# Splitting w_o in the queue of the other late weights, beside the w_in products, instead of in the chunk stage

## The chip, the cores and the metric

The kernel runs on one core of a Trainium2 chip. A core has a matrix engine (TensorE, PE in the profile), a vector engine (VectorE, DVE), a scalar engine (ScalarE, ACT), GpSimd (POOL) and SyncE (SP), which here only issues transfers. Each engine works through its own list of instructions in order. Transfers are issued from the lists of SP and ACT (SPq and ACTq in the profile) and run on 16 shared DMA engines. The metric is the device time of one execution in microseconds, the median of several runs.

## The reference, cut to what matters

One layer of a decoder is computed for a prompt of 1024 rows and for 64 sample rows (8 sequences of 8):

```
h = rmsnorm(x) * (1 + scale) + shift
[u_pool | z_pool | z_ssm | xBC | dt | g] = h @ w_in
P = (pool_mix(u_pool) * silu(z_pool)) @ w_pool_out        # 512 -> 1024
S = gated_rmsnorm(SSD(conv(xBC)) + D*x, z_ssm) @ w_ssm_out # 2048 -> 1024
x = x + gate * ((sigmoid(g_pool) * P + sigmoid(g_ssm) * S) @ w_o)   # w_o: 1024 x 1024
y = rmsnorm(x)
```

All data are float32. SSD is a state recurrence that runs over chunks of 128 rows, for four groups of heads.

## The kernel before, in words

**Halves.** A product of full accuracy is made of three products of rounded numbers: each weight tile is split into a high half (the rounded tile) and a low half (the tile less its rounded self), and each activation likewise; then high x high, high x low and low x high are accumulated. ACT makes the high half by a copy, and GpSimd makes the low half by a subtraction.

**Stages.** In the profile's time the stages follow one another like this.
- Up to about 95 us: the norm, the modulation, the first products (`first`).
- 95 to about 535 us: 20 pairs of column blocks of w_in (`pair`, `strassen`): each pair is seven products on PE, and after each product `run_units` calls `beside` once; that is one step. In this stage the pairs belong to the convolution and the pooling (DVE does their element work), with some plain gates between them. For each pair ACT and GpSimd also split seven w_in tiles (`split`, lines 155 to 163; tiles `whi` and `wlo`, four buffers each); their raw data arrive in `rawA` by SP's queue.
- 535 to about 800 us: ten more pairs of w_in, with the sample rows' recurrence beside them.
- About 830 to 1110 us: the chunk stage. 32 chunks (4 groups x 8) are woven with 32 product units (`pieces`) that multiply by w_pool_out and by three quarters of w_ssm_out; PE's list is written out in order there.
- From 1110 us: the last quarter of w_ssm_out, the gates, and the product with w_o.

**The queue of late weights.** `splits` (lines 408 to 447) splits the weights that are needed only in the chunk stage or after it and puts both halves into DRAM: 8 tiles of w_pool_out and 32 of w_ssm_out, each 128 x 512. A job has three parts. `begin` takes a buffer `pw` (two exist) and loads the raw tile by ACT's queue. `halve` makes the high half on ACT into the buffer `ph` (one exists) and stores it by ACT's queue, then the low half on GpSimd in place in `pw`; a tile of w_ssm_out is scaled by four ACT instructions first. `end` stores the low half by SP's queue. Job n begins at step 17n/5, is halved three steps and ended five steps after that. The steps are those of the 20 pairs between 95 and 535 us. A transfer that waits for a buffer or for data holds everything behind it in the list of its engine.

**w_o.** `wo_splits` (lines 1663 to 1677) does the same for w_o in the chunk stage: 16 tiles of 128 x 512, the raw tile loaded by SP's queue, the high half made on ACT and stored by ACT's queue, the low half made on GpSimd and stored by SP's queue. Two raw buffers and one `ph` exist here as well. It is called twice for each chunk from chunk 13 on, and what the lists' planner makes of that lies between 840 and 992 us. `wo_prep` loads the halves back from DRAM after 1130 us.

**Order.** A planner orders the instructions of each engine from the order of the program, priorities and estimated times; `behind` and `paced` tie some transfers and copies to earlier instructions.

Of the kernel before, what the change touches and what calls it, by code (L numbers as in the profile page):

```python
# [8 lines left out]
F32 = mybir.dt.float32  # L9
F32R = mybir.dt.float32r  # L10
AF = mybir.ActivationFunctionType
ALU = mybir.AluOpType
# [8 lines left out]
P = 128  # L21
D = 1024
# [7 lines left out]
NG = 4  # L30
# [16 lines left out]
def tile_pool_ssd_step(  # L47
# [6 lines left out]
    nc = tc.nc  # L54
    uid = [0]

    def nm(s):
        uid[0] += 1
        return f"{s}_{uid[0]}"
# [45 lines left out]
    load = nc.sync.dma_start  # L105
    store_ = nc.scalar.dma_start
    mm = nc.tensor.matmul
    act = nc.scalar.activation
# [225 lines left out]
    def in_line(engines, begin=False):  # L334
        traced = nc.cur_bb.bb.instructions
        for i in traced[len(traced) if begin else line[0]:]:
            if i.engine in engines:
                if i.engine in line[1]:
                    tc.add_manual_dep(i, line[1][i.engine], mybir.DependencyInfo(
                        mybir.DependencyClass.NoSync, mybir.DependencyReason.DATA), reason="in_line")  # L340
                line[1][i.engine] = i.name
        line[0] = len(traced)
# [42 lines left out]
    def dram(name, shape, dt=F32):  # L385
        return dr.tile(list(shape), dt, tag=name, name=name)
# [10 lines left out]
    wp_d = [dram(f"wp{m}", [P, 2, 4, P]) for m in range(8)]  # L397
    ws_d = [[dram(f"ws{g}{m}", [P, 2, 4, P]) for m in range(8)] for g in range(NG)]

    def behind(engine, n=0):  # L400

        of = (i for i in reversed(nc.cur_bb.bb.instructions) if i.engine == engine)
        for _ in range(n):
            next(of)
        return tc.issue_after(next(of))


    def splits():
        jobs = [(w_pool_out[0, :, m * P:(m + 1) * P], None, wp_d[m]) for m in range(8)]
        jobs += [(w_ssm_out[0, g * 512:(g + 1) * 512, m * P:(m + 1) * P], 24 + 4 * g, ws_d[g][m])  # L410
                 for g in range(NG) for m in range(8)]
        raws, made = {}, [0]

        def paced():

            return highs[min(made[0] + 3, len(highs) - 1)]

        def begin(n):
            raws[n] = gas[0].tile([P, 4, P], F32, tag="pw", name=nm("pw"), bufs=2)
            with tc.issue_after(paced()):  # L420
                store_(raws[n], jobs[n][0].rearrange("(k p) c -> p k c", p=P))

        def halve(n):
            raw, gain = raws[n], jobs[n][1]
            hi = gas[0].tile([P, 4, P], F32R, tag="ph", name=nm("ph"), bufs=1)
            with tc.issue_after(paced()):
                if gain is not None:
                    for k in range(4):
                        act(raw[:, k], raw[:, k], AF.Copy, scale=vT[:, gain + k:gain + k + 1])
                act(hi, raw, AF.Copy)  # L430
                store_(jobs[n][2][:, 0], hi.bitcast(F32))
            nc.gpsimd.tensor_tensor(raw.bitcast(F32R), raw, hi.bitcast(F32), ALU.subtract)

        def end(n):
            with behind(mybir.EngineType.SP):
                load(jobs[n][2][:, 1], raws.pop(n))
        at = {}
        for n in range(len(jobs)):
            for f, step in ((end, 5), (begin, 0), (halve, 3)):
                at.setdefault(n * 17 // 5 + step, []).append((f, n))  # L440
        for t in range(max(at) + 1):
            made[0] += 1
            for f, n in sorted(at.get(t, ()), key=lambda x: x[1]):
                f(n)
            yield
# [254 lines left out]
    def between(n):  # L700
        with behind(mybir.EngineType.DVE):
            if n != 3:
                step()
            if n in (3, 4, 5) and prep_q:
                next(prep_q[0], None)
            while n == 6 and later:
                step()
# [32 lines left out]
    gas = []  # L740
# [634 lines left out]
    def sample_end(g):  # L1375
        sz = ckt([P, 4, P], "sz", 3)[:, :, :NS]
        load(sz, z_d[g][:, :, SEQ:])
        v = ckt([P, 4, P], "v")[:, :, :NS]
        load(v, ys_d[g])
        finish(g, SEQ, NS, v, sz)  # L1380
# [148 lines left out]
    def pool_rows():  # L1529
        with behind(mybir.EngineType.SP):  # L1530
            load(new_pool_s[0, :, 0:7, :], state_pool[0, :, 8:15, :])

    first()
    units = [plain(to_conv), light[1], plain(pool_rows)]
    units += weave(heavy, light[2:-LAST])
    pre = splits()
    units.append(plain(lambda: [None for _ in pre]))
    units.append(plain(to_ssd))
# [64 lines left out]
    ck = right.__enter__()  # L1603
# [48 lines left out]
    def pieces():  # L1652
        ws = first_ws
        nxt = len(ws)
        for i, (pf, run) in enumerate(prods):
            while nxt < len(prods) and nxt <= i + 1:
                ws[nxt] = prods[nxt][0]()
                nxt += 1
            yield from run(ws.pop(i))
    pc_ = pieces()  # L1660
    wo_d = [dram(f"wo{k}", [P, 2, D]) for k in range(8)]

    def wo_splits():
        raws = {}
        for n in range(18):
            if n < 16:
                raws[n] = ck.tile([P, 512], F32, tag="pw", name=nm("pw"), bufs=2)
                load(raws[n], w_o[0, n // 2 * P:n // 2 * P + P, n % 2 * 512:n % 2 * 512 + 512])
            if n > 1:
                load(wo_d[(n - 2) // 2][:, 1, n % 2 * 512:n % 2 * 512 + 512], raws.pop(n - 2))  # L1670
            yield
            if n < 16:
                hi = ck.tile([P, 512], F32R, tag="ph", name=nm("ph"), bufs=1)
                act(hi, raws[n], AF.Copy)
                store_(wo_d[n // 2][:, 0, n % 2 * 512:n % 2 * 512 + 512], hi.bitcast(F32))
                nc.gpsimd.tensor_tensor(raws[n].bitcast(F32R), raws[n], hi.bitcast(F32), ALU.subtract)
            yield
    wos = wo_splits()
    RATE = 2.56
    FRONT = 4  # L1680

    def products(t):

        nonlocal made
        while made < RATE * t:
            next(pc_, None)
            made += 1
# [5 lines left out]
        next(pc_)  # L1693
    next(seq[0])
    for i in range(len(seq)):
        if i > 12:
            next(wos, None)
        if i + 1 < len(seq):
            with behind(mybir.EngineType.DVE, 1 - i) if i < 2 else ExitStack():
                next(seq[i + 1])  # L1700
        products(i + 0.4)
        if i > 0:
            next(seq[i - 1], None)
        if i > 12:
            next(wos, None)
        next(seq[i], None)
        if i % NC == 3:
            sample_end(i // NC)
        if i + 3 < len(seq):
            next(seq[i + 3])  # L1710
        if i + 2 < len(seq):
            with behind(mybir.EngineType.Activation) if i == 0 else ExitStack():
                next(seq[i + 2])
        products(i + 1.0)
    next(seq[-1], None)
    for it in (pc_, wos):
        for _ in it:
            pass
    in_line((mybir.EngineType.PE,))
    right.__exit__(None, None, None)  # L1720
    while right_all:
# [16 lines left out]
    for c in range(9):  # L1738
        n = min(P, T - c * P)
# [5 lines left out]
    for c in range(9):  # L1745
        n = min(P, T - c * P)
# [4 lines left out]
    wo, mh, ml = [None] * 8, [None] * 8, [None] * 8  # L1751
# [90 lines left out]
    for half in range(2):  # L1842
        c = slice(half * 512, half * 512 + 512)
# [102 lines left out]
```

## Time and profile before

| | |
|---|---|
| median of 3 runs | 1297.37 us (1296.57 to 1301.63) |
| span of the profiled execution, first to last instruction | 1297.1 us |
| granted clock of PE, mean over the span | 0.999 |
| busy PE / DVE / ACT / POOL | 1255.9 / 910.5 / 708.8 / 677.4 us |
| moved by DMA | 251.70 MB, mean 194 GB/s |

The profile is that of one execution. Its span is the time that it gives for that execution. The page lists busy time by engine, the span in slices, the DMA queues, the chain of work that ended last, and groups of instructions by source line. Views of the same trace give busy time in chosen stretches, what each engine waited for, single instructions in order of time, and all instructions that touch a tile. In a row of single instructions the numbers are start, duration, engine, line, operation and shape; what stands in brackets is the idle time of the engine before it and what ended it. In a row of a tile the numbers are the count, then shortest, median and longest duration in ns, then first and last start.

### The profile page before, as it was taken

The numbers are of one execution on the slowest core, as the hardware profiler recorded it, in microseconds if no ns is written. First come the engines' busy times: TensorE is split into PE (matmuls) and PEld (weight loads), VectorE is DVE, ScalarE is ACT, GpSimd is POOL, SyncE is SP. The second block draws the span as 40 slices with busy tenths as digits, with TensorE's granted clock in tenths as the row PEclk, the third lists the DMA queues.
The fourth block names the chain that finished last, engine by engine and source line by source line (L and its number), as shares of the span: only waits on it lengthen the run. The fifth ranks groups of instructions, "written<-read, shape, count | busy, mean of one in ns | idle before, by whom it ended". The sixth has DMA issues, their size and how long they took to land.

```text
span 1297.1 us, 26554 instructions
## 1 busy us (share of the span) xinstructions
PE 1255.9 (97%) x9771; PEld 1173.9 (90%) x9771; DVE 910.5 (70%) x1580; ACT 708.8 (55%) x1684; POOL 677.4 (52%) x563
## 2 busy tenths in 40 slices
PE   7999999999999999999999999999998999999998
PEld 6779999989999999999889999889998999999786
DVE  4685778866979578775777665488676888576433
ACT  4665356375656564545455453687987868201111
POOL 1007668677869776664344444276776747314000
PEclk9999999999999999999999999999999999999999
DMA  9837345465455544444656555999988656575631
GB/s 326 259 107 224 119 150 173 142 202 170 146 180 197 165 155 133 161 135 129 181 158 173 152 178 164 356 355 354 338 270 262 202 168 199 172 266 159 226 106 52
DMA packets 233795, 251.70 MB, mean 194 GB/s; under 512 B 31265, under 2 KB 177905, under 8 KB 233658
## 3 DMA queue, kind: packets, MB, share of 16 engines
q1 hardware_dynamic: 161568, 171.60, 42.1%
q10 hardware_dynamic: 72098, 78.41, 17.5%
q8 instruction: 77, 1.26, 0.4%
q14 instruction: 52, 0.43, 0.1%
HBM read 167.06 MB, written 83.01 MB: 193 GB/s over the span
## 4 chain that ended last, share of the span: by engine, by line
PE 67%; issue 8%; DMA 8%; DVE 6%; POOL 5%; ACT 4%; SPq 0%; ACTq 0%; POOLq 0%; DVEq 0%
PE ps L603 6%; PE ps L604 6%; PE ps L605 6%; PE mm L603 6%; PE mm L605 6%; PE mm L604 6%; PE mm L355 3%; PE mm L356 3%; PE mm L354 3%; PE ps L1208 2%; PE ps L1892 2%; PE ps L1894 2%; PE ps L1893 2%; POOL wlo L163 2%; PE ps L1211 2%
## 5 line engine op out<-in xcount | busy, mean ns | idle before, releaser
L163 POOL TENSOR_TENSOR wlo<-rawA,whi 128x512 fp32r<-128x512 f32 x120 | 184.0, 1538 | 185.6 <-ACT whi L160 101.6
L163 POOL TENSOR_TENSOR wlo<-raw,whi 128x512 fp32r<-128x512 f32 x92 | 150.7, 1646 | 125.3 <-ACT whi L160 91.1
L354 PE MATMUL mm<-Y,whi 128*128 128x352 f32 (+1 forms) x480 | 160.1, 334 | 0.7 <-DVE G L1795 0.5
L355 PE MATMUL mm<-Y,whi 128*128 128x352 f32 (+1 forms) x480 | 157.3, 328 | 1.0 <-DVE Y L1466 1.0
L356 PE MATMUL mm<-Y,wlo 128*128 128x352 f32 (+1 forms) x480 | 156.9, 327 | 0.0
L605 PE MATMUL mm<-Y,wlo 128*128 128x272 f32 x496 | 143.6, 290 | 3.9 <-POOL wlo L163 3.1
L603 PE MATMUL ps<-Y,whi 128*128 128x272 f32 x496 | 144.5, 291 | 2.3 <-ACT o L803 1.7
L603 PE MATMUL mm<-Y,whi 128*128 128x272 f32 x496 | 146.5, 295 | 0.2
L604 PE MATMUL ps<-Y,whi 128*128 128x272 f32 x496 | 143.1, 289 | 0.0
L604 PE MATMUL mm<-Y,whi 128*128 128x272 f32 x496 | 142.9, 288 | 0.0
L605 PE MATMUL ps<-Y,wlo 128*128 128x272 f32 x496 | 142.6, 288 | 0.0
L160 ACT ACTIVATE whi<-rawA 128x512 fp32r<-128x512 f32 x125 | 78.2, 626 | 95.6 <-PE ps L604 44.9
L1051 DVE SCALAR_TENSOR_TENSOR GA<-GA,cvT,GA 128x1112 f32<-128x1112 f32 x72 | 127.1, 1769 | 0.6 <-ACT GA L1048 0.5
L160 ACT ACTIVATE whi<-raw 128x512 fp32r<-128x512 f32 x96 | 58.7, 626 | 91.4 <-DVE raw L549 41.7
L605 PEld LDWEIGHTS mm<-Y,wlo 128*128 128x128 f32 x496 | 93.4, 188 | 5.8 <-POOL wlo L163 4.2
L603 PEld LDWEIGHTS ps<-Y,whi 128*128 128x128 f32 x496 | 93.3, 188 | 4.0 <-ACT o L803 1.9
L603 PEld LDWEIGHTS mm<-Y,whi 128*128 128x128 f32 x496 | 93.3, 188 | 2.5 <-issue 0.8
L604 PEld LDWEIGHTS mm<-Y,whi 128*128 128x128 f32 x496 | 93.4, 188 | 0.7 <-issue 0.6
L604 PEld LDWEIGHTS ps<-Y,whi 128*128 128x128 f32 x496 | 93.3, 188 | 0.3 <-issue 0.2
L605 PEld LDWEIGHTS ps<-Y,wlo 128*128 128x128 f32 x496 | 93.4, 188 | 0.2 <-issue 0.2
L354 PEld LDWEIGHTS mm<-Y,whi 128*128 128x128 f32 x480 | 90.3, 188 | 3.2 <-DVE G L1795 1.4
L355 PEld LDWEIGHTS mm<-Y,whi 128*128 128x128 f32 x480 | 90.3, 188 | 3.2 <-DVE Y L1466 1.6
(452 smaller groups left out, 3851.6 us busy)
## 6 DMA issues: line engine op xcount, KB each, us to landing
rawA<-in_w_in SPq DMA_DIRECT2D x46, 512.0 KB
dec<-acs_d SPq DMA_DIRECT2D x32, 512.0 KB
xbc<-GA ACTq DMA_DIRECT2D x24, 512.0 KB
xb<-xbc SPq DMA_DIRECT2D x32, 384.0 KB
rawA<-in_w_in SPq DMA_DIRECT2D x32, 256.0 KB
pw<-in_w_ssm_out ACTq DMA_DIRECT2D x32, 256.0 KB
ws<-ph ACTq DMA_DIRECT2D x32, 256.0 KB
ws<-pw SPq DMA_DIRECT2D x32, 256.0 KB
```

The source lines that it names most:

```text
L160: ins = act(hi[:, :, :ncols], raw[:, :, :ncols], AF.Copy)
L163: (eng or nc.gpsimd).tensor_tensor(lo[:, :, :ncols], raw[:, :, :ncols], hi[:, :, :ncols].bitcast(F32), ALU.subtract)
L354: mm(ps[:, :n], a, rh[k][:, o:o + n], start=(k == 0), stop=False)
L355: mm(ps[:, :n], a, rl[k][:, o:o + n], start=False, stop=False)
L356: mm(ps[:, :n], b, rh[k][:, o:o + n], start=False, stop=(k == nk - 1))
L603: mm(p, hi, ah, start=(k == 0), stop=False)
L604: mm(p, hi, al, start=False, stop=False)
L605: mm(p, lo, ah, start=False, stop=(k == 3))
L1051: V.scalar_tensor_tensor(d[:, :n], rp[:, k:k + n], cvT[:, 24 * k + mc:24 * k + mc + 1], d[:, :n], ALU.mult, ALU.add)
L1208: mm(o[hh], xd[:S, 2 * q + hh, :], dec[:S, 2 * q + hh], start=True, stop=state is None)
L1211: mm(o[hh], state[:, h * 64:h * 64 + 64], cE[:, h], start=False, stop=True)
L1892: mm(ps[:, :cw], mhk, wo[k][0][:, s], start=(k == 0), stop=False)
```

## The change

The 16 tiles of w_o become the last 16 jobs of `splits`, behind the 40 that are there. The jobs are spread at 12/5 steps each in place of 17/5, so that the 56 jobs take about as many steps as the 40 did. There are three raw buffers `pw` in place of two. The raw tiles of w_o are thus loaded by ACT's queue and no longer by SP's; the other parts of a job run on the same engines as before. `wo_splits` and its calls in the chunk stage are gone. [...] The other buffers and the loads of the halves after 1130 us stay as they are. The list of PE holds the same instructions; in eight places before the chunk stage neighbouring products have changed places.

```diff
@@ splits
-        jobs = [(w_pool_out[0, :, m * P:(m + 1) * P], None, wp_d[m]) for m in range(8)]
-        jobs += [(w_ssm_out[0, g * 512:(g + 1) * 512, m * P:(m + 1) * P], 24 + 4 * g, ws_d[g][m])
-                 for g in range(NG) for m in range(8)]
+        def tiles(src):
+            return src.rearrange("(k p) c -> p k c", p=P)
+
+        def half(t, n):
+            return t[..., n * 512:n * 512 + 512].rearrange("p (k c) -> p k c", c=P)
+
+        jobs = [(tiles(w_pool_out[0, :, m * P:(m + 1) * P]), None, [wp_d[m][:, j] for j in range(2)]) for m in range(8)]
+        jobs += [(tiles(w_ssm_out[0, g * 512:(g + 1) * 512, m * P:(m + 1) * P]), 24 + 4 * g,
+                  [ws_d[g][m][:, j] for j in range(2)]) for g in range(NG) for m in range(8)]
+        jobs += [(half(w_o[0, k * P:(k + 1) * P], n), None, [half(wo_d[k][:, j], n) for j in range(2)])
+                 for k in range(8) for n in range(2)]
...
-            raws[n] = gas[0].tile([P, 4, P], F32, tag="pw", name=nm("pw"), bufs=2)
+            raws[n] = gas[0].tile([P, 4, P], F32, tag="pw", name=nm("pw"), bufs=3)
...
-                at.setdefault(n * 17 // 5 + step, []).append((f, n))
+                at.setdefault(n * 12 // 5 + step, []).append((f, n))
@@ chunk stage
-    wo_d = [dram(f"wo{k}", [P, 2, D]) for k in range(8)]
-
-    def wo_splits():
...
-    wos = wo_splits()
...
-        if i > 12:
-            next(wos, None)
...
@@ kernel
-    nc = _bacc.Bacc("TRN2", target_bir_lowering=False, num_devices=1)
+    nc = _bacc.Bacc("TRN2", target_bir_lowering=False, num_devices=1, dynamic_dma_scratch_size=1024)
```

More of the change, by code (lines that the diff above doesn't have):

```diff
@@ L398, in tile_pool_ssd_step @@
     ws_d = [[dram(f"ws{g}{m}", [P, 2, 4, P]) for m in range(8)] for g in range(NG)]
+    wo_d = [dram(f"wo{k}", [P, 2, D]) for k in range(8)]
     def behind(engine, n=0):
@@ L418, in begin @@
         def begin(n):
-            raws[n] = gas[0].tile([P, 4, P], F32, tag="pw", name=nm("pw"), bufs=2)
+            raws[n] = gas[0].tile([P, 4, P], F32, tag="pw", name=nm("pw"), bufs=3)
             with tc.issue_after(paced()):
-                store_(raws[n], jobs[n][0].rearrange("(k p) c -> p k c", p=P))
+                store_(raws[n], jobs[n][0])
         def halve(n):
@@ L430, in halve @@
                 act(hi, raw, AF.Copy)
-                store_(jobs[n][2][:, 0], hi.bitcast(F32))
+                store_(jobs[n][2][0], hi.bitcast(F32))
             nc.gpsimd.tensor_tensor(raw.bitcast(F32R), raw, hi.bitcast(F32), ALU.subtract)
@@ L435, in end @@
             with behind(mybir.EngineType.SP):
-                load(jobs[n][2][:, 1], raws.pop(n))
+                load(jobs[n][2][1], raws.pop(n))
         at = {}
@@ L1660, in tile_pool_ssd_step @@
     pc_ = pieces()
-    wo_d = [dram(f"wo{k}", [P, 2, D]) for k in range(8)]
-    def wo_splits():
[L1664 to L1677, printed above, removed]
-    wos = wo_splits()
     RATE = 2.56
@@ L1703, in tile_pool_ssd_step @@
             next(seq[i - 1], None)
-        if i > 12:
-            next(wos, None)
         next(seq[i], None)
@@ L1715, in tile_pool_ssd_step @@
     next(seq[-1], None)
-    for it in (pc_, wos):
-        for _ in it:
-            pass
+    for _ in pc_:
+        pass
     in_line((mybir.EngineType.PE,))
```

## The prediction

> **What bounds the kernel now.** I read the page first, then busy time by stretch, then what TensorE (PE) waited for in the two stretches that the change touches, then single instructions there.
>
> ```profile
> span 1297.1 us, 26554 instructions
> PE 1255.9 (97%) x9771; PEld 1173.9 (90%) x9771; DVE 910.5 (70%) x1580; ACT 708.8 (55%) x1684; POOL 677.4 (52%) x563
> ...
> q1 hardware_dynamic: 161568, 171.60, 42.1%
> q10 hardware_dynamic: 72098, 78.41, 17.5%
> ```
>
> PE is busy for 97% of the span, so whatever moves on the other engines can change the time only through the 41.2 us (1297.1 - 1255.9) in which PE stands still. The profiled span of 1297.1 us is 0.3 us under the median of the runs, 1297.37 us; I sum against the span and carry the difference to the median. About 0.5%, 6.5 us, is what the runs (1296.57 to 1301.63) let a measurement tell from no change.
>
> The next view is busy time by stretch. 95 to 535 us holds the w_in products of the convolution and pooling pairs, where 40 split jobs run already; 838 to 1000 us is the part of the chunk stage in which w_o is split; 1000 to 1110 us is the same stage without that.
>
> ```profile
> 95.00:310.00 215.00, 210.90 (x1650) 206.67 (x1649) 156.07 (x249) 116.28 (x272) 155.46 (x98) 1.00 0.52 168
> 310.00:535.00 225.00, 224.26 (x1768) 221.06 (x1768) 178.26 (x261) 132.44 (x319) 173.94 (x102) 1.00 0.51 164
> 838.00:1000.00 162.00, 153.28 (x1260) 141.56 (x1259) 124.70 (x185) 133.34 (x365) 109.49 (x117) 1.00 0.96 318
> 1000.00:1110.00 110.00, 109.63 (x916) 101.57 (x915) 93.88 (x149) 82.07 (x226) 69.25 (x84) 1.00 0.60 179
> ```
>
> Columns: length, then busy PE, PEld, DVE, ACT, POOL, the granted clock (full in all four rows), DMA share, GB/s. PE idles 4.1 us in the first row, 0.7 in the second, 8.7 in the third (162 - 153.28) and 0.4 in the fourth. The third has its DMA engines full at 0.96 and ACT at 82%. So at most some 8 us are to be won there, and 4.8 us of idle time show how the front copes with 40 jobs. Most of what PE waited for in the front (us in total, times, longest):
>
> ```profile
> PE mm L605 <- POOL wlo L163: 2.6, 4, 0.8
> PE ps L603 <- ACT o L803: 1.7, 1, 1.7
> ```
>
> **What leaves the chunk stage.** All that touches the w_o buffers there:
>
> ```profile
> L1668 SPq DMA_DIRECT2D pw<-in_w_o x16: 332/402/2769, 839.9 to 984.2; - x16
> L1674 ACT ACTIVATE ph<-pw x16: 615/624/644, 847.2 to 988.5; 128x512 fp32r<-128x512 f32 x16
> L1676 POOL TENSOR_TENSOR pw<-pw,ph x16: 1266/1292/1809, 847.9 to 989.3; 128x512 fp32r<-128x512 f32 x16
> L1670 SPq DMA_DIRECT2D wo<-pw x16: 319/354/965, 849.2 to 992.4; - x16
> L1675 ACTq DMA_DIRECT2D wo<-ph x16: 326/326/389, 847.8 to 989.2; - x16
> ```
>
> That is 16 x 0.624 = 10.0 us of ACT, 16 x 1.29 = 20.7 us of POOL, 16 x (0.402 + 0.354) = 12.1 us of SP's queue, 16 x 0.326 = 5.2 us of ACT's queue, and 16 x 3 x 256 KB = 12.6 MB. None of it is on PE; it costs time where it makes something late that PE waits for. These rows show how:
>
> ```profile
> 981.30 0.63 ACT L1674 ACTIVATE ph<-pw 128x512 fp32r<-128x512 f32 x1 [2.75 <-DMA wo<-ph]
> ...
> 989.20 0.59 ACT L1415 ACTIVATE xw<-ps 128x512 fp32r<-128x512 f32 x1
> ```
>
> ```profile
> 983.19 0.50 PE L1429 MATMUL ps<-xw,bt 128*128 128x512 f32 x1 [2.05 <-DVE xwl L1419]
> ...
> 991.75 0.44 PE L1208 MATMUL ps<-dec,xd 128*64 128x128 f32 x4 [0.89 <-DVE dec L1416]
> 992.88 0.44 PE L1211 MATMUL ps<-cE,hst 128*64 128x128 f32 x4 [0.69 <-DVE cE L1418]
> ```
>
> The one ph buffer is still being stored when the next half is to be made, ACT stands for 2.75 us (L1674 makes the half), the chunk's xw behind it is late, then DVE's xwl, and PE stops for 2.05 us. The next chunk's xw (L1415), with one more half ahead of it, starts only at 989.20 us; behind it PE stops for 0.89 + 0.69 = 1.58 us. Two more stops:
>
> ```profile
> 857.18 0.44 PE L1208 MATMUL ps<-dec,xd 128*64 128x128 f32 x4 [1.40 <-DVE dec L1416]
> 858.40 0.44 PE L1211 MATMUL ps<-cE,hst 128*64 128x128 f32 x4 [0.78 <-POOL Y L1373]
> 962.54 0.44 PE L1211 MATMUL ps<-cE,hst 128*64 128x128 f32 x4 [0.79 <-DVE cE L1418]
> ```
>
> ```profile
> 841.79 0.97 SPq L1668
> 842.85 7.48 DMA xb<-xbc
> ```
>
> In the chain of waits the 2.18 us (1.40 + 0.78) near 857 go back to an xb load that was issued behind a w_o load and took 7.48 us on full DMA engines. I count half, 1.1 us, since the engines are full before w_o begins, too. Ahead of the 0.79 us stands this:
>
> ```profile
> 957.31 0.68 DVE L1438 TENSOR_TENSOR hst<-hst,ps 128x512 f32<-128x512 f32 x1
> 957.91 1.63 DVE L1362 TENSOR_TENSOR v<-v,sz 128x512 f32<-128x512 f32 x1
> ```
>
> ```profile
> 957.68 1.30 POOL L1676 TENSOR_TENSOR pw<-pw,ph 128x512 fp32r<-128x512 f32 x1
> ```
>
> DVE's v product takes 1.63 us where the neighbour of the same size takes 0.68, and is over 0.6 us after the w_o subtraction is. That 0.95 us more than covers PE's 0.79, which I count whole. The sum is 2.05 + 1.58 + 1.1 + 0.79 = 5.5 us. Its ends: 0 if other late work takes the places (PE's order in this stage is the same in the changed program, but ACT, POOL, DVE and SP are reordered around it), and 8.2 us if this stretch becomes as clean as 1000 to 1110 us (8.7 less 0.4 x 162 / 110). I take 5.5, as its rows name w_o.
>
> [...]
>
> **What the front takes on.** Sixteen more jobs beside the same 20 pairs, one per 2.4 steps in place of one per 3.4. Its jobs now:
>
> ```profile
> L429 ACT ACTIVATE pw<-pw,vT x128: 384/387/406, 180.1 to 520.5; 128x128 f32<-128x128 f32 x128
> L430 ACT ACTIVATE ph<-pw x40: 613/624/636, 103.4 to 523.9; 128x512 fp32r<-128x512 f32 x40
> L432 POOL TENSOR_TENSOR pw<-pw,ph x40: 1272/1296/2385, 104.5 to 524.6; 128x512 fp32r<-128x512 f32 x40
> L421 ACTq DMA_DIRECT2D pw<-in_w_ssm_out x32: 386/390/668, 177.1 to 515.0; - x32
> L436 SPq DMA_DIRECT2D ws<-pw x32: 319/344/897, 188.4 to 526.0; - x32
> ```
>
> A w_o job has no scaling: 0.624 us of ACT, 1.296 of POOL, 0.390 + 0.326 of ACT's queue (its load moves from SP to ACT), 0.344 of SP's. Times 16: 10.0, 20.7, 11.5 and 5.5 us over 440 us. DMA rises from 73.0 MB (168 GB/s x 215 us + 164 x 225) to 85.6, the share from 0.515 to 0.60, at which 1000 to 1110 us left PE only 0.4 us idle. The denser pace also moves the scaled ssm_out jobs forward. By 310 us about 30 jobs will have been halved where about 20 are now, nearly all of the extra ones scaled: 10 x (4 x 0.387 + 0.624) = 22 us more ACT, to 138 of 215 us (64%), and 13 to 24 us more POOL, to 168 to 179 of 215 (78 to 83%). In the second stretch the w_o jobs without scales make ACT lighter, and POOL gets up to 8 us more on 174 of 225. Neither becomes the bound; what can hurt is lateness of single wlo or whi tiles. PE lost 4.8 us beside 40 jobs, 0.12 us a job, so 16 more cost 1.9 us. Ends: a gain of 1.7 us, if the third raw buffer removes the wait for L803, and a loss as in the second rival below.
>
> That the third buffer need not remove it is seen here:
>
> ```profile
> 218.47 2.37 POOL L432 TENSOR_TENSOR pw<-pw,ph 128x512 fp32r<-128x512 f32 x1
> ```
>
> ```profile
> 242.68 1.45 SPq L436 DMA_DIRECT2D ws<-pw  x2
> ```
>
> ```profile
> 248.92 0.63 ACT L160 ACTIVATE whi<-rawA 128x512 fp32r<-128x512 f32 x1 [4.79 <-DMA ws<-pw]
> ```
>
> A low half was ready at 220.84 us, but its store stood in SP's queue, behind loads that wait for buffers of their own, until 242.68. So the raw buffer came free late, ACT stood for 4.79 us at the next load, and the 1.7 us that PE waited for L803 came out of it (266 us, by the chain of waits). In the order of the changed program three such stores stand behind that place and three loads in a row on ACT.
>
> The smaller scratch I cost at nothing: the two dynamic queues above are issued by SP and ACT, and no data transfer is issued from POOL. No row prices it; an effect would show at all transfers alike.
>
> Sum: -5.5 + 1.9 = -3.6 us, a span of 1293.5 us and a median of 1293.8 us.
>
> **Rivals.** (1) The chunk stage becomes clean and the front costs nothing: 1297.4 - 8.2 = 1289.2 us. For it: the idle rate after 1000 us. Against it: of the 8.7 us some 2.1 (8.7 less the 6.6 of the six stops shown) have no w_o in their chain. Chance 0.22. (2) Slower: SP's holds. ACT blocks at raw loads as at 248 us.
>
> ```profile
> SPq L1027 <- PE ps L1033: 42.9, 7, 10.0
> ```
>
> SP stood 7 times at such a load between 95 and 535 us (up to 10.0 us). If each hold blocks ACT with three loads queued, PE loses between 1.7 us, what the one at 248 cost it, and 4.79 us, ACT's whole stop, at each: 11.9 to 33.5 us, so 1297.4 - 5.5 + 11.9 = 1303.8 up to 1325 us. It decides once the front loses over 12.0 us (5.5 + 6.5) more than now. Against it: the other six cost PE nearly nothing so far. Chance 0.15. (3) The w_o stops are replaced by others, as the stage is tight in DVE and ACT: 0 gained, 1.9 lost, 1299.3 us. Chance 0.19. [...] Chance 0.04. [...]
>
> **How the numbers follow.** Forecast 0.40, range 1291 to 1297 us. With the rivals: faster than 1290.9 us 0.22 (rival 1), slower than 1303.9 us 0.19 (rivals 2 and 4), the rest 0.59 (the forecast and rival 3). The range 1288.5 to 1304 us takes in rival 1 with a little front gain, rival 3 and the low edge of rival 2.
>
> **What would show it.** Right: PE idle in the chunk stage's w_o stretch falls from 8.7 to about 3 us, DMA share there from 0.96 to about 0.75 (12.6 of 51.6 MB gone, by the 318 GB/s over 162 us), no ACT stop of 2.75 us; front idle rises from 4.8 to about 6.7 us. Wrong: ACT idle before L160 behind stores of pw adds up to tens of us, or waits for wlo in the front exceed 12 us, or the chunk waits for dec and cE stay at 5 us and more.

## The result, and the profile after

The changed kernel is slower: 1306.03 us median (1302.39 to 1311.1, 8 runs) beside 1297.97 us of the kernel before (1291.09 to 1301.63, 8 runs), a ratio of 1.0069 with a 95% interval of 1.0046 to 1.0091. The profiled execution is the fastest of the eight (1302.39 us, span 1300.6 us, mean clock 0.997), so its trace shows only 3.5 of the about 8 us.

The page of the changed kernel:

```profile
span 1300.6 us, 26519 instructions
PE 1259.1 (97%) x9771; PEld 1176.0 (90%) x9771; DVE 907.4 (70%) x1580; ACT 708.7 (54%) x1684; POOL 680.5 (52%) x563
```

PE executes the same 9771 instructions, is busy for 3.2 us longer and stands for 41.5 us (1300.6 - 1259.1) in place of 41.2. Busy time by stretch in the changed kernel (length, then busy PE, PEld, DVE, ACT, POOL, the granted clock, DMA share, GB/s):

```profile
95.00:310.00 215.00, 208.64 (x1613) 203.78 (x1612) 154.78 (x249) 125.14 (x307) 160.27 (x103) 0.99 0.61 196
310.00:535.00 225.00, 223.00 (x1749) 218.79 (x1747) 177.49 (x260) 124.43 (x290) 184.10 (x108) 1.00 0.58 190
838.00:1000.00 162.00, 157.11 (x1285) 145.47 (x1285) 120.96 (x184) 127.69 (x354) 87.69 (x101) 1.00 0.78 256
```

PE now idles 6.4 and 2.0 us in the two rows of the front (before 4.1 and 0.7) and 4.9 us in the chunk stage's row (before 8.7). Fixed stretches understate the loss, since the later kernel has fewer instructions in them. With the same some 2200 instructions of PE between the ends, first the kernel before, then the changed one:

```profile
177.30:460.60 283.30, 279.75 (x2203) 275.32 (x2202) 224.91 (x332) 165.67 (x402) 222.23 (x129) 1.00 0.53 171
```

```profile
176.80:468.10 291.30, 283.47 (x2202) 277.31 (x2201) 223.75 (x330) 175.11 (x429) 235.12 (x140) 0.99 0.60 196
```

The changed kernel needs 8.0 us more for them: 4.3 us more standing (283.3 - 279.75 = 3.55 us before, 291.3 - 283.47 = 7.83 us after) and 3.7 us more "busy". At the start of the chunk stage it is 7.9 us behind in the trace (the same instruction of PE begins at 840.5 us instead of 832.7), it wins 4 us there and loses nothing further: at the end it is 3.5 us behind.

The largest single loss of the front, in the list of SP of the changed kernel (start, duration, line, transfer, number):

```profile
236.10 1.15 SPq L1037 DMA_DIRECT2D stc<-in_state_conv  x3
246.62 0.39 SPq L545 DMA_DIRECT2D rawA<-in_w_in  x1
247.06 1.55 SPq L446 DMA_DIRECT2D ws<-pw  x3
```

on ACT:

```profile
247.00 0.62 ACT L160 ACTIVATE whi<-rawA 128x512 fp32r<-128x512 f32 x1
252.34 1.86 ACTq L431 DMA_DIRECT2D pw<-in_w_ssm_out  x3
257.67 1.28 ACT L439 ACTIVATE pw<-pw,vT 128x128 f32<-128x128 f32 x4 [10.06 <-DMA pw<-in_w_ssm_out]
...
263.30 0.63 ACT L440 ACTIVATE ph<-pw 128x512 fp32r<-128x512 f32 x1 [2.14 <-DMA ws<-ph]
263.84 0.61 ACT L160 ACTIVATE whi<-raw 128x512 fp32r<-128x512 f32 x1
```

and on PE:

```profile
264.51 0.39 PE L613 MATMUL mm<-Y,whi 128*128 128x272 f32 x1 [2.11 <-ACT whi L160]
264.74 0.28 PE L614 MATMUL mm<-Y,whi 128*128 128x272 f32 x1
266.56 0.59 PE L615 MATMUL mm<-Y,wlo 128*128 128x272 f32 x1 [1.54 <-POOL wlo L163]
...
267.18 0.43 PE L614 MATMUL ps<-Y,whi 128*128 128x272 f32 x1
```

Read from the top: SP stands for 9.3 us at the rawA load (L545), which waits until 246.62 us for its buffer; what ends the wait is a wlo subtraction on GpSimd (L163). Three low halves (L446) are queued behind it and leave at 247.06. All three raw buffers are held by them, so the next three raw loads on ACT (L431) begin only at 252.34 us, and ACT stands for 10.06 us with the splits of w_in for the running products queued behind it. They come at 263.84 us; PE stops for 2.11 and 1.54 us; and then its matmuls take 0.43 us in place of 0.28 for 3.4 us:

```profile
266.00:269.00 3.00, 2.44 (x11) 2.44 (x12) 0.00 (x0) 3.00 (x9) 3.00 (x4) 0.52 0.53 167
```

The granted clock is 0.52 there (0.50 from 266.12 to 269.54 us). Half speed for 3.4 us costs 1.7 us, which is part of the 3.7 us "busy" more; the rest of it the profile does not separate. By the same instructions of PE in the two traces, this place costs 4.6 us (the changed kernel is 1.9 us behind at 259 us and 6.4 at 263), of which 1.9 go again, as the kernel before has a stop of its own near 266; the rest of the 8.0 us comes in smaller steps near 196, 237 and 405 to 426 us.

Most of what PE waited for in the second stretch of the front, and in the chunk stage to 1000 us (us in total, times, longest):

```profile
PE mm L615 <- POOL wlo L163: 1.3, 2, 1.0
```

```profile
PE ps L1218 <- DVE dec L1426: 2.2, 2, 1.7
PE ps L1221 <- DVE cE L1428: 1.9, 3, 0.8
PE mm L355 <- POOL Y L1383: 0.7, 1, 0.7
```

The 2.05 us wait for xwl is gone; dec, cE and Y are still late. One stop of these is new. In the kernel before ACT stores the last state of a group of heads (L1451) and comes to the next xD, which takes the same buffers, 7 us later without a wait:

```profile
916.45 0.42 ACTq L1451 DMA_DIRECT2D out<-xD  x1
...
918.03 2.44 ACT L1196 ACTIVATE dec<-dec,acT 128x128 f32<-128x128 f32 x8
...
921.43 1.06 ACT L1392 ACTIVATE cE<-dec 128x1024 f32<-128x1024 f32 x1 [0.24 <-PE ps L1211]
...
922.55 0.62 ACT L1674 ACTIVATE ph<-pw 128x512 fp32r<-128x512 f32 x1
923.07 0.59 ACT L1415 ACTIVATE xw<-ps 128x512 fp32r<-128x512 f32 x1
...
923.75 1.28 ACT L1423 ACTIVATE xD<-xb,Dv 128x128 f32<-128x128 f32 x4
```

Between the two, ACT makes dec, cE and xw of the chunk that follows, and one half of w_o (0.62 us). In the changed kernel the planner has put that cE, xw and dec behind the xD; ACT comes to the xD early and waits for the store:

```profile
922.78 0.40 ACTq L1461 DMA_DIRECT2D out<-xD  x1
...
930.00 1.28 ACT L1433 ACTIVATE xD<-xb,Dv 128x128 f32<-128x128 f32 x4 [3.88 <-DMA out<-xD]
...
932.64 0.59 ACT L1425 ACTIVATE xw<-ps 128x512 fp32r<-128x512 f32 x1
```

Behind it PE stops where the kernel before does not:

```profile
935.13 0.44 PE L1218 MATMUL ps<-dec,xd 128*64 128x128 f32 x4 [0.43 <-DVE dec L1426]
936.36 0.44 PE L1221 MATMUL ps<-cE,hst 128*64 128x128 f32 x4 [0.78 <-DVE cE L1428]
```

### The profile page after: what moved, and what is told of

Read it like the earlier page. It is cut to its first block, busy times and chain, and to the rows that moved or that the text cites. A ratio compares the mean times of both kernels' runs of the same rounds, so it can differ in the third digit from the quotient of the medians.

```text
span 1300.6 us, 26519 instructions
## 1 busy us (share of the span) xinstructions
PE 1259.1 (97%) x9771; PEld 1176.0 (90%) x9771; DVE 907.4 (70%) x1580; ACT 708.7 (54%) x1684; POOL 680.5 (52%) x563
## 4 chain that ended last, share of the span: by engine, by line
PE 60%; DMA 8%; ACT 5%; DVE 4%; issue 3%; POOL 2%; ACTq 1%; SPq 0%; DVEq 0%; POOLq 0%
PE ps L613 5%; PE ps L614 5%; PE ps L615 5%; PE mm L613 5%; PE mm L615 5%; PE mm L614 5%; PE mm L354 4%; PE mm L355 4%; PE mm L356 4%; PE ps L1879 2%; PE ps L1881 2%; PE ps L1880 2%; PE ps L1218 2%; PE ps L1221 2%; POOL wlo L163 1%
## 5 line engine op out<-in xcount | busy, mean ns | idle before, releaser
L163 POOL TENSOR_TENSOR wlo<-rawA,whi 128x512 fp32r<-128x512 f32 x120 | 184.9, 1544 | 180.8 <-ACT whi L160 97.9
L163 POOL TENSOR_TENSOR wlo<-raw,whi 128x512 fp32r<-128x512 f32 x92 | 153.7, 1678 | 104.9 <-ACT whi L160 74.0
L354 PE MATMUL mm<-Y,whi 128*128 128x352 f32 (+1 forms) x480 | 160.1, 334 | 0.6 <-DVE G L1782 0.5
L1061 DVE SCALAR_TENSOR_TENSOR GA<-GA,cvT,GA 128x1112 f32<-128x1112 f32 x72 | 124.4, 1731 | 4.7 <-ACT GA L1058 4.6
L442 POOL TENSOR_TENSOR pw<-pw,ph 128x512 fp32r<-128x512 f32 x56 | 88.6, 1582 | 29.0 <-ACT ph L440 28.7
L613 PEld LDWEIGHTS mm<-Y,whi 128*128 128x128 f32 x496 | 93.4, 188 | 4.9 <-ACT whi L160 3.3
L614 PEld LDWEIGHTS mm<-Y,whi 128*128 128x128 f32 x496 | 93.4, 188 | 0.7 <-issue 0.6
L355 PEld LDWEIGHTS mm<-Y,whi 128*128 128x128 f32 x480 | 90.3, 188 | 4.2 <-DVE Y L1476 1.6
```

The lines of the kernel that those rows point to most:

```text
L163: (eng or nc.gpsimd).tensor_tensor(lo[:, :, :ncols], raw[:, :, :ncols], hi[:, :, :ncols].bitcast(F32), ALU.subtract)
L354: mm(ps[:, :n], a, rh[k][:, o:o + n], start=(k == 0), stop=False)
L355: mm(ps[:, :n], a, rl[k][:, o:o + n], start=False, stop=False)
L613: mm(p, hi, ah, start=(k == 0), stop=False)
L614: mm(p, hi, al, start=False, stop=False)
L1061: V.scalar_tensor_tensor(d[:, :n], rp[:, k:k + n], cvT[:, 24 * k + mc:24 * k + mc + 1], d[:, :n], ALU.mult, ALU.add)
```

## The experiments

The theory after the result: the denser pace with three raw buffers makes ACT stand behind SP's hold, and the w_o jobs as such cost little. The rivals: sixteen more jobs are too much work for ACT or POOL, or bring too many subtractions beside DVE's work (in the kernel before DVE's v product takes 1.63 us beside the one at 957.68 us, and 0.69 at 845.53 with nothing on GpSimd); the chunk stage or the new placement of tiles takes the gain back. A second theory came up with the first run below: that without w_o a wait appears in the chunk stage that was not there before. The ratios are to the kernel before, with 95% intervals.

**The chunk stage alone.** The kernel before with nothing split there:

```diff
-    wos = wo_splits()
...
-        if i > 12:
-            next(wos, None)
...
-        load(hi.bitcast(F32), wo_d[k][:, 0])
-        load(lo.bitcast(F32), wo_d[k][:, 1])
+        load(hi.bitcast(F32), w2_d[k][:, 0].rearrange("p g k c -> p (g k c)"))
+        load(lo.bitcast(F32), w2_d[k][:, 1].rearrange("p g k c -> p (g k c)"))
```

`w2_d` holds halves of w_ssm_out, two groups of `ws_d` laid side by side.

> The kernel before without any splitting of w_o: wo_splits is left out, and the last product loads halves of w_ssm_out of the same size in its place, so y is not the reference's. It measures what the chunk stage gives when w_o leaves it, with the front as it was. By the trace of the changed kernel the chunk stage gives 3.6 to 4 us (its lead over PE's list falls from +7.9 to +3.9): 1294 us where before is 1298, ratio 0.997. If the gain of that one execution is not typical, ratio 1.000.

Measured: 1298.76 us (12 runs), ratio 1.0008 (0.9993 to 1.0022): between -0.9 and +2.9 us, no gain of 5.5. But in its trace the stops that the forecast was made of are gone: 0.27 and 0.79 us stand near 857, nothing between 940 and 1000 us. In their place there is this, on ACT and then on PE:

```profile
912.76 0.40 ACTq L1453 DMA_DIRECT2D out<-xD  x1
...
921.65 1.28 ACT L1425 ACTIVATE xD<-xb,Dv 128x128 f32<-128x128 f32 x4 [5.02 <-DMA out<-xD]
...
924.28 0.58 ACT L1417 ACTIVATE xw<-ps 128x512 fp32r<-128x512 f32 x1
```

```profile
926.77 0.44 PE L1210 MATMUL ps<-dec,xd 128*64 128x128 f32 x4 [1.76 <-DVE dec L1418]
928.00 0.54 PE L1213 MATMUL ps<-cE,hst 128*64 128x128 f32 x4 [0.79 <-DVE cE L1420]
```

The store of the last state holds a buffer of xD, ACT waits 5.02 us for it, dec and cE come late and PE stops for 1.76 + 0.79 = 2.55 us. ACT's list has the order of the changed kernel here: the next xw stands behind the xD. It is the same in every kernel that ran: all ten with no w_o in the chunk stage and with the shared buffer have this order, and ACT waits 3.8 to 5.5 us at this xD; the four with w_o there have dec, cE and xw between the store and the xD, and no wait. So the order hides the wait, by the chunk's own 2.44 + 1.06 + 0.59 us in the kernel before; the half of w_o in between is 0.62 us. Behind PE's two stops the granted clock falls, to a mean of 0.57 over 4 us (3.4 of them at one half):

```profile
928.00:932.00 4.00, 4.00 (x31) 3.52 (x32) 1.34 (x4) 3.19 (x7) 2.41 (x4) 0.57 0.44 154
```

That makes a cause that can be tried: the same kernel with a buffer of its own for that output.

```diff
-            fo = ckt([P, 4, P], "xD")
+            fo = ckt([P, 4, P], "fo", 1)
```

> The kernel before with no w_o split at all (the last product takes halves of w_ssm_out in its place, so the result leaves out w_o), and the output tile of the last state (fo, line 1451 of the kernel before) in a buffer of its own in place of one of the two xD buffers. PE's list is the same. Theory: the 5.5 us of stops go when w_o leaves the chunk stage, but ACT, no longer busy with w_o, then reaches the next xD while its buffer is still being stored (5.02 us of waiting, then 1.76 + 0.79 us of PE stops and a half-clock stretch of 3.4 us, some 4 us); with a buffer of its own that is gone and the time is 1298.0 - 4 = about 1294 us, ratio 0.996 to 0.998, PE idle from 838 to 1000 us 2 to 3 us. Rival, the stops of the one execution meant nothing for the median: ratio 1.000 as without the buffer.

Measured: 1294.81 us (12 runs), ratio 0.9961 (0.9942 to 0.9981), which is -5.1 us (0.0039 x 1299.19, the median of the kernel before on the chip of this run). No wait for such a store is left on ACT, and what PE still waited for from 838 to 1000 us is

```profile
PE ps L1210 <- DVE dec L1418: 1.4, 2, 1.1
PE mm L355 <- POOL Y L1375: 1.2, 1, 1.2
PE ps L1213 <- POOL Y L1375: 0.8, 1, 0.8
```

3.5 us of idle time in that row where 2 to 3 were expected (a wait for Y of 1.2 us is new). So the stops that w_o caused are worth about what was forecast, and a wait that the new order of ACT's list brings took them back. ACT waits for two more such stores later (1.51 and 6.62 us in the kernel before, 2.43 and 6.44 without w_o), and the new buffer removes these too; PE stands for only 0.33 us behind them in the kernel before. The kernel before with the new buffer alone was not run. How much of the 5.1 us is this wait is less exact: at the same instruction of PE near 1010 us the two profiled executions lie 2.7 us apart, while the ratios differ by 0.0047, 6 us, with some 3 us of uncertainty (both intervals together). The new buffer also let the planner move a few instructions of ACT and DVE around it.

**Pace and amount.** The changed kernel without the w_o jobs (the last product takes other halves, as above), once at the old pace and once at the new:

```diff
-        jobs += [(half(w_o[0, k * P:(k + 1) * P], n), None, [half(wo_d[k][:, j], n) for j in range(2)])
-                 for k in range(8) for n in range(2)]
...
-                at.setdefault(n * 12 // 5 + step, []).append((f, n))
+                at.setdefault(n * 17 // 5 + step, []).append((f, n))
```

The second hunk stands in the first of the two kernels only.

> As the run without the splitting of w_o, but out of the changed kernel: 40 jobs at the old pace of 17/5 steps, three raw buffers, small scratch. Theory buffers (ACT stands at raw loads and at the one ph buffer, and the denser pace makes that worse): nothing lost, ratio to before 0.995 to 0.998, front idle of PE at most the 4.8 us of before. Theory scratch (the smaller scratch slows transfers): 1.003 or more.

> The changed kernel with its pace of 12/5 steps, three raw buffers and small scratch, but without the 16 w_o jobs (left out as in the run without splitting, so y is not the reference's); the 40 jobs end after some 100 steps. Theory pace (the scaled jobs packed closer make ACT stand at 190 to 290 us): most of the front's loss stays, ratio to before 1.000 to 1.004, a half-clock stretch of PE near 265 us. Theory amount (it is the 16 more jobs): ratio 0.996 to 0.998.

Measured: 1293.03 us at the old pace (6 runs, ratio 0.9949, 0.9929 to 0.9969); 1309.18 us at the new (6 runs, ratio 1.0073, 1.0051 to 1.0095). The same 40 jobs at another pace: 16 us, more than either theory gave (1.000 to 1.004 was the higher range). The changed kernel, with the w_o jobs, has 1306.03: the sixteen jobs add nothing measurable to what the pace costs. By the same instruction of PE at the start of the chunk stage (832.8 us in the kernel before), the third buffer at the old pace wins 5.3 us, and the new pace then loses 13.9; the changed kernel's 7.9 us behind is of that size. The front at the old pace, third buffer included:

```profile
95.00:310.00 215.00, 214.42 (x1687) 211.14 (x1686) 161.36 (x254) 119.22 (x278) 159.96 (x99) 1.00 0.54 172
310.00:535.00 225.00, 225.00 (x1775) 221.88 (x1772) 179.91 (x263) 129.89 (x313) 172.90 (x102) 1.00 0.51 165
```

PE idles 0.6 us in 440 (4.8 in the kernel before). At the new pace ACT's list shows the same stop as the changed kernel, with no w_o job in the program:

```profile
259.55 1.28 ACT L439 ACTIVATE pw<-pw,vT 128x128 f32<-128x128 f32 x4 [10.03 <-DMA pw<-in_w_ssm_out]
```

and behind it half the clock again, for longer (a mean of 0.57 over 8 us):

```profile
266.00:274.00 8.00, 6.08 (x27) 5.87 (x28) 0.00 (x0) 8.00 (x22) 7.35 (x6) 0.57 0.59 188
```

**Buffers.** The changed kernel with a second `ph`, and with four or six raw buffers:

```diff
-                hi = ...tile([P, 4, P], F32R, tag="ph", name=nm("ph"), bufs=1)
+                hi = ...tile([P, 4, P], F32R, tag="ph", name=nm("ph"), bufs=2)
```

> The changed kernel with two ph buffers. Theory single ph (ACT stands 14.5 us for ws<-ph stores at the dense pace): most of the loss goes, 1295 to 1299 us, ratio 0.998 to 1.001. Theory raw buffers (ACT's 10.06 us stop at 257 us): little goes, 1303 to 1306 us, ratio 1.004 to 1.007.

```diff
-            raws[n] = gas[0].tile([P, 4, P], F32, tag="pw", name=nm("pw"), bufs=3)
+            raws[n] = gas[0].tile([P, 4, P], F32, tag="pw", name=nm("pw"), bufs=6)
```

> The changed kernel with six raw buffers and the one ph. Theory raw buffers: most of the loss goes, 1295 to 1299 us, ratio 0.998 to 1.001. Theory single ph: 1303 to 1306 us, ratio 1.004 to 1.007. If both are needed, both runs stay above 1.002.

> The changed kernel with four raw buffers (three: 1306 us, six: 1294.7 us). Theory raw buffers by count (at 12/5 steps a job, a buffer held over one stop of SP's queue of some 15 to 20 us needs two or three more than the steps ask for): between, 1297 to 1301 us, ratio 0.999 to 1.002. If the fourth already takes the stop at 257 us away: 1294 to 1296 us. If the gain of six came from another order of instructions: 1303 us or more.

> The changed kernel with six raw buffers in place of three and three ph buffers in place of one. Theory buffers: ACT's waits for ws<-ph stores and for raw loads in 95 to 310 us (14.5 and 12.4 us) go to under 5 together, no PE stop of 2 us there, ratio to before 0.995 to 0.999. Theory amount (ACT, GpSimd and DMA have too much to do at this pace): ratio 1.004 to 1.008 as the changed kernel's 1.007.

| kernel | median us | ratio (95%) |
|---|---|---|
| changed kernel, pw 3, ph 1 | 1306.03 | 1.0069 (1.0046 to 1.0091) |
| pw 3, ph 2 | 1303.68 | 1.0029 (1.0011 to 1.0048) |
| pw 4, ph 1 | 1296.07 | 0.9975 (0.9959 to 0.9992) |
| pw 6, ph 1 | 1294.65 | 0.9963 (0.9945 to 0.998) |
| pw 6, ph 3 | 1294.19 | 0.9965 (0.9951 to 0.998) |

Most of the loss hangs on the raw buffers: by the medians one more takes 10.0 us off (1306.03 - 1296.07) and three more 11.4, by the ratios 12 and 14; the second `ph` takes 2.4 or 5. With 1.0029 the second `ph` lies between the ranges of its two theories, and one raw buffer more brings nearly all, where the first theory gave an intermediate time. What ACT waited for at the first scaling, with two `ph` and then with four `pw`:

```profile
ACT pw L439 <- DMA pw<-in_w_ssm_out: 12.7, 3, 10.2
```

```profile
ACT pw L439 <- DMA pw<-in_w_ssm_out: 2.1, 2, 1.4
```

The ten-microsecond stop stays with the one and is gone with the other. The front with six raw buffers:

```profile
95.00:310.00 215.00, 213.86 (x1674) 209.78 (x1673) 158.53 (x253) 132.02 (x318) 173.99 (x108) 1.00 0.63 202
310.00:535.00 225.00, 225.00 (x1776) 221.87 (x1775) 186.18 (x263) 124.54 (x289) 190.09 (x109) 1.00 0.59 191
```

PE idles 1.1 us in all, with all 56 jobs there and POOL busier than in the kernel before (174 and 190 us against 155 and 174). Of GpSimd's subtractions for wlo and pw between 95 and 535 us, 65 of 196 take over 2 us here where most take 1.3; in the changed kernel it is 54 of 191, in the kernel before 52 of 179. So neither the amount of work nor these long subtractions cost the time in the changed kernel. The versions with four or six raw buffers beat both kernels.

The version with six raw buffers and one `ph`, with the buffer of its own for the last state as above:

> The changed kernel with six raw buffers and the same buffer of its own for the last state; the whole computation. Theory of the xD store: its trace without this buffer has ACT waiting 4.63 us at xD, PE stopping for 1.18 us behind it and a half-clock stretch of 3.4 us, some 3 us: 1294.65 - 3 = about 1292 us, ratio 0.993 to 0.995. Rival, stops of one execution mean nothing for the median: 1294 to 1295 us, ratio 0.996.

Measured: 1291.93 us (5 runs), ratio 0.9939 (0.9924 to 0.9953). This is the fastest complete kernel. It lies 0.0024 (3 us) under the ratio without the new buffer, about as expected; the uncertainty of that difference is 0.0023 (both intervals together).

**Is there more to be had from other steps?** Six raw buffers and three `ph`; first with more lead between the parts of a job, then with the 40 scaled jobs spread wider and the w_o jobs packed behind them:

```diff
-            for f, step in ((end, 5), (begin, 0), (halve, 3)):
+            for f, step in ((end, 7), (begin, 0), (halve, 5)):
```

> Six raw buffers and three ph buffers, and each job halved five steps after its load and its low half stored seven steps after (three and five before). If ACT's waits for raw loads that have not landed still cost something at six and three buffers: 1290 to 1293 us, ratio 0.993 to 0.996. If the front has no such cost left: 1294 us, ratio 0.996 to 0.998, as with six and three buffers alone.

```diff
-                at.setdefault(n * 12 // 5 + step, []).append((f, n))
+                at.setdefault(min(n, 40) * 14 // 5 + max(n - 40, 0) * 3 // 2 + step, []).append((f, n))
```

> Six raw buffers and three ph buffers, the 40 scaled and pooling jobs at 14/5 steps and the 16 w_o jobs at 3/2. Theory amount (what is left of the front's cost is ACT and GpSimd work packed too closely between 190 and 310 us): 1291 to 1293 us, ratio 0.994 to 0.996. Theory buffers alone: 1294 us, ratio 0.996 to 0.998.

Measured: 1294.33 us (12 runs, 0.9964, 0.9948 to 0.998), no more than without the lead; and 1298.15 us (12 runs, 0.9985, 0.9969 to 1.0001), some 4 us worse and above what both theories gave. What PE waited for between 515 and 540 us in the last:

```profile
PE mm L615 <- POOL wlo L163: 3.8, 1, 3.8
```

Where the w_o jobs are packed at 1.5 steps, a wlo tile is late, and the trace falls from 1.0 us ahead of the one with six and three buffers alone to 4.6 us behind. But by 834 us it is only 1.4 us behind, and the 4.7 us that it loses after that lie at stops in the chunk stage that both traces have and that half the clock follows in this one (behind the 1.99 us at 931.29 us the matmuls of L1218 take 0.70 us in place of 0.44; the mean clock from 838 to 1000 us is 0.97). How much of the 4 us is the density stays open; that the w_o jobs cost nothing is shown for 2.4 steps only.

**Scratch and third buffer in the kernel before.** Its w_o splitting stays in the chunk stage; first both, then the scratch alone. The scratch is what `dynamic_dma_scratch_size` sets; at 1024 it leaves 15 KB more of each partition to the tiles, as the pad further below shows (3840 float32), and a third `pw` takes 2 KB (512 float32).

```diff
-            raws[n] = gas[0].tile([P, 4, P], F32, tag="pw", name=nm("pw"), bufs=2)
+            raws[n] = gas[0].tile([P, 4, P], F32, tag="pw", name=nm("pw"), bufs=3)
...
-    nc = _bacc.Bacc("TRN2", target_bir_lowering=False, num_devices=1)
+    nc = _bacc.Bacc("TRN2", target_bir_lowering=False, num_devices=1, dynamic_dma_scratch_size=1024)
```

> The kernel before with the third raw buffer and the smaller scratch, and nothing else: the old pace, w_o split in the chunk stage. Theory third buffer (ACT's stops at raw loads cost the front its 4 to 5 us): 1292 to 1294 us, ratio 0.995 to 0.997, as in the run with three buffers and no splitting of w_o. If w_o out of the chunk stage is needed for that gain: 0.999 to 1.002.

> The kernel before with the smaller scratch alone. If the scratch has no part, as every transfer is issued by SP and ACT: ratio 0.998 to 1.002. If it has (by addresses of tiles or in another way): outside of that, and the gain given to the third buffer is its own.

Measured: 1304.25 us with both (12 runs, 1.0036, 1.0019 to 1.0053) and 1308.44 us with the scratch alone (6 runs, 1.0071, 1.0045 to 1.0098). Both expectations were missed. In the front the third buffer does what was expected: with both, PE is 4.2 us ahead at the start of the chunk stage (832.8 us in the kernel before) and idles 0.6 us from 95 to 535 us. The loss comes behind it. What PE waited for between 836 and 870 us with the scratch alone, and a stretch of that kernel just ahead:

```profile
PE ps L1208 <- DVE dec L1416: 9.3, 2, 5.4
```

```profile
800.00:838.00 38.00, 36.38 (x269) 35.53 (x265) 13.23 (x26) 20.88 (x38) 17.71 (x12) 1.00 0.99 345
```

PE stands for 9.3 us, in two stops, and half the clock follows each: behind the 3.94 us at 841.36 us the matmuls of L354 take 0.52 us in place of 0.34, behind the 5.37 us at 864.53 those of L1208 take 0.67 to 0.69 in place of 0.44, and the mean clock from 862 to 872 us is 0.66. The chain of waits says what came first:

```profile
809.42 8.44 DMA pw<-in_w_o
...
819.84 7.36 DMA wlo<-wp
```

The first two w_o loads are issued at 799.40 and 809.42 us, the kernel before issues its first at 839.9; the DMA engines are full (0.99), and loads that the first chunks need come behind. Nothing in the source of the chunk stage differs. With the smaller scratch the tiles have other addresses, and by the order of the two traces the planner put some 55 instructions of ACT, 39 of SP, 23 of POOL and 13 of DVE in other places, and none of PE. The next kernel parts the two: scratch of 1024 bytes, with an unused tile ahead that leaves every other tile where it was:

```diff
+    pad = const([P, 3840], "pad")
+    nc.gpsimd.memset(pad[:, 0:1], 0.0)
...
+    nc = _bacc.Bacc(..., dynamic_dma_scratch_size=1024)
```

> The kernel before with the smaller scratch and, first of all tiles, an unused tile of 15 KB per partition, so that every other tile stands at the address that it has in the kernel before; the lists of PE, DVE, ACT and SP are then those of before, and POOL has one small memset more. Theory placement (the smaller scratch alone was 0.7% slower because the tiles moved, the planner could start the w_o loads earlier, and the chunk stage's first loads waited behind them): ratio 0.998 to 1.002. Theory scratch (transfers themselves are slower): 1.005 to 1.009, as with the smaller scratch alone.

Measured: 1299.35 us (12 runs), ratio 0.9997 (0.9982 to 1.0012). The lists of PE, DVE, ACT and SP are the kernel before's, POOL has one memset more, and the time is the same: the size of the scratch costs nothing, the new placement does, as long as w_o is split in the chunk stage. That the cost comes by the early w_o loads is read from the chain and was not tried by itself.

The padded kernel is also a second look at the kernel before, since four of its lists are equal. Its last stops before 1000 us:

```profile
984.42 0.50 PE L1431 MATMUL ps<-xw,bt 128*128 128x512 f32 x1 [0.32 <-DVE xwl L1421]
992.98 0.44 PE L1210 MATMUL ps<-dec,xd 128*64 128x128 f32 x4 [0.89 <-DVE dec L1418]
994.11 0.44 PE L1213 MATMUL ps<-cE,hst 128*64 128x128 f32 x4 [0.69 <-DVE cE L1420]
```

The 0.89 and 0.69 us come back to the hundredth; the 2.05 us for xwl are 0.32 here.

## Why the prediction was wrong

**The chunk stage, -5.5 us: the stops went as described, and another took their place.** Taking w_o out measures 0 (-0.9 to +2.9 us), and -5.1 us once the wait at xD is taken out as well. So the rows were read rightly (but for the 2.05 us, which vary), and what failed is the question that each removed stall needs: what is late next. The text asked it only as an end of the range, "0 if other late work takes the places", and took 5.5 "as its rows name w_o". This end is what came, by the third rival's mechanism. The text knew that ACT's list is reordered when the halves leave, and did not ask what the new order brings: the xD ahead of the next chunk's cE, xw and dec, and so a wait for the store that shares its buffers. In the changed kernel's trace the replacement was small (0.43 + 0.78 us) and the stage won 4 us.

**The front, +1.9 us: mis-sized by a factor of over four, and for a reason that the term did not hold.** It took 0.12 us for each of sixteen jobs. The jobs measure nothing; the pace that the change gives all jobs costs 16 us against the same 40 jobs at the old pace, both with three buffers. In the trace the same instructions take 8.0 us longer. An average of the idle time over the jobs says nothing of the next pace, as each further job in SP's hold takes a raw buffer until there is none.

**"The third buffer need not remove" the wait for L803: right for the new pace only.** The row at 242.68 us showed the mechanism as it then struck: low halves stuck behind SP's hold. At the old pace three buffers were enough, and PE's idle time in the front fell to 0.6 us. At the new pace three halves stand behind the hold, and three buffers are as few as two were. The text even counted them, three stores and three loads in a row, and then gave the case 0.15.

**Rival 2 was the right mechanism with the wrong account.** SP's hold blocks ACT at raw loads: yes, but the hold that cost most is one of 9.3 us (to 246.6), not seven, and at a rawA load that waits for GpSimd, not at the loads of the state (L1027) that the text counted. Half the clock, which follows some of PE's stops (3.41 us of it those of 2.11 and 1.54 us), was not in its price. It decided earlier than "once the front loses over 12.0 us", because the 5.5 us that it had to eat up first were mostly not there; that the median (1306.03) lies in its span of 1303.8 to 1325 is luck, since neither seven holds nor the 5.5 us are in it.

**The scratch at nothing: right for the transfers, blind for the placement.** The size alone cost nothing (0.9997 with every other tile at its old address); that it would was the author's estimate. In the kernel before, the new addresses alone cost 0.7%. In the changed kernel the w_o load that did the damage is no longer in that stage. What the placement does to the changed kernel was not tried.

**Held:** the DMA share of the chunk stretch (0.78, foreseen 0.75), no 2.75 us stop of ACT there, idle falling (to 4.9, foreseen 3), neither ACT nor POOL the bound (125 and 160 of 215 us in the first stretch, where 138 and 168 to 179 were foreseen), and the low chance of rival 4, that the moved subtractions hold up DVE. Its 0.04 rests on a length that no run shows, a subtraction's whole 1.29 us: the v product at 957.91 us took 0.95 us more, and with six buffers the same subtractions are in the front and PE idles 1.1 us. The sign named as wrong, ACT standing behind the stores of pw, is what came, as one stop of 10.06 us.

Of the about 7.4 us between the spans of the two kernels (medians 1296.9 of 81 executions and 1304.3 of 8), the mean clock (0.9964 and 0.9946) accounts for 2.3 (0.0018 x 1304), and about 5 are left for the stops.

## What to carry to other kernels

Work that is taken out of a planned list changes the order of what stays: compare the engine's list before and after, and look for waits that are new, first at buffers that a store shares with later work. Size the buffers of a queue for the longest hold of the engine that frees them, counted in jobs at the new pace, not by an average cost of a job. A change of a reserved size moves addresses and with them a planner's order; a pad that keeps the addresses tells the two apart.

## What the hardware showed that was not expected

A short stop of PE can cost more than itself. In fourteen profiled executions (95 to 1280 us) I compared PE's stops with the stretches in which the granted clock is one half. Such a stretch lasts 3.4 us (266.12 to 269.54 us in the changed kernel), or 6.8 (within 266 to 274 us at the new pace without the w_o jobs). 26 of 29 begin within about 2 us of a stop of at least 1 us; the other three lie at 1135 to 1149 us. Stops of 1.0 to 1.5 us were followed by one in 2 of 44 cases, of 1.5 to 2 us in 8 of 23, of 2 to 3 us in 13 of 19, over 3 us in 5 of 5. So in these executions a stop of 2 to 3 us cost, more often than not, another 1.7 us (half of 3.4). How much clock is lost differs between runs of one kernel: of the 12 runs with nothing split in the chunk stage and the buffer of its own, the two fastest (1288.75 and 1289.19 us) have a mean clock of 0.999 and the slowest (1298.99 us) 0.995.

The length of one stop alone does not decide it. In the kernel before the clock stays at 1.00 behind the stop of 2.40 us that ends at 666.26 us and the one of 2.05 us that ends at 983.19, and in the changed kernel behind the one of 2.30 us that ends at 673.97; there the one stretch at half the clock between 95 and 1280 us begins at 266.12 us, behind the 2.11 us that end at 264.51 us and within the 1.54 us that end at 266.56. What decides between these cases was not shown.
